# Decay sums broadcast through memory, forget columns third in the order of blocks, and first loads in one queue

## The chip, the cores and the metric

One core of a Trainium2 chip runs the whole program. The metric is the device time of one execution in microseconds (us): the median over three runs, 729.85 us for the kernel before. The profile comes from a single execution, which took 731.11 us.

## The reference, cut to what matters

Two blocks run one after the other on 256 rows of 1024 channels, all in float32: first a feed-forward layer, a chunked attention with pooling and a second feed-forward layer, then a forgetting attention ("fox") and a sparse latent attention ("dsa"). What the change touches in the arithmetic is the forgetting attention:

```python
q, k, v, f_logit, gate = _split(x @ w_in, [H * dh, H * dh, H * dh, H, D])
log_f = jax.nn.log_sigmoid((f_logit + b_f).astype(jnp.float32))
cum = jnp.cumsum(log_f, axis=1)
cum_t = jnp.transpose(cum, (0, 2, 1))
...
s = jnp.einsum('bqhd,bshd->bhqs', q_b, k).astype(jnp.float32) * scale
s = s + jnp.transpose(c_b, (0, 2, 1))[..., None] - cum_t[:, :, None, :]
s = jnp.where(kpos[None, :] <= qpos[:, None], s, -jnp.inf)
p = jax.nn.softmax(s, axis=-1).astype(v.dtype)
```

There are 8 heads of 128 channels. The score of query q and key k gets the decay sum of q, minus the decay sum of k, and a causal mask.

## The kernel before, in words

**Work and tiles.** The 256 rows are two tiles of 128 (t = 0 and 1). Every weight matrix is read once from memory, in units listed in order by `unit_list`: a unit is two blocks of 128 x 512 values (the first 8 units of all are one block each). A unit is loaded into `raw` (L209, 4 buffers) by the queue of SyncE (SP), and split by `prefetch` (L185 to L201) into a rounded part `whi` on ScalarE (ACT, L196) and the rest `wlo` on VectorE (DVE, L197), 8 buffers each. Activations are split alike (`xh`, `xl`). TensorE (PE) forms a float32 product as three fast ones: `half` (L214 to L228) issues, for each block, xl by whi, xh by wlo and xh by whi. Some small products (scores of tile 0, probabilities by values) are done in plain float32, which the profile records as two matmuls each.

**Order of the work.** `Kern` writes the instructions in one order, with side work put off: `later` and `when` push a function on a heap with a due time counted in modelled TensorE time (`now`, advanced by `mm` and `tr`), and `pump` runs what is due after each `half`. The due times stand in `DUE`. The framework's scheduler then orders the instructions of each engine by readiness in its own model; each engine runs its list strictly in that order.

**Start.** `start` (L1097) loads the channel gains by the GpSimd (POOL) queue (L1100), and by the SP queue, in turn, weights and two blocks of the transposed input `xin` (L1102 to L1104). TensorE does 40 products of zeros (L1107). `first_chunk` (L310) multiplies two blocks of `xin` by the gain into `xg` on DVE (L321), rounds it on ACT (`xh`, L324), subtracts on DVE (`xl`, L325), and issues the units. The input `x` itself, needed for the norm, is loaded after the second and fourth pair of blocks (`X_AT`, L333).

**Feed-forward.** Gate and up chunks of 512 columns alternate; the gated result is transposed through memory by POOL's queue (`regroup`, L281 to L282: `d<-hb`, then `hd<-d`), and `put_h` splits it (L238, L239) `DUE["ffn_T"]` = 6.0 after that.

**Forgetting attention** (`fox`, L687). Columns of the input projection come in the order of `FOX_CH`: two chunks of keys, two of queries, three `fox_fv` chunks of 344 (the 8 forget columns, then the values), two of gates. After the first `fox_fv` chunk `log_f` and then `cums` (L752) make the decay sums: `cq` per query row (L763), and per key in `cum`, 40 rows with the sums rounded in rows 0 to 7 and the rest in rows 32 to 39. In `scores` (L782) each head begins with a product that adds the key's decay sum to its scores in PSUM: 40 rows of a column of `E`, repeated 128 times, by `cum` (L788); then the q k products (L790, L792); then DVE adds `cq` and the mask (L793):

```python
self.mm(ps[:, i, :], E[:, h:h + 1].to_broadcast([40, P]), cum[:, 0:nk], True, False, 1)
```

There are six groups of heads (`GROUPS`): two of 4 heads for tile 0 with 128 keys, four of 2 heads for tile 1 with 256 keys. Each goes through softmax (L443, L445), a transpose (L178), the product with the values and the gate (L868), while TensorE does the gate chunks and `out_proj`.

Of the kernel before, what the change touches and what calls it, by code (L numbers as in the profile page):

```python
# [31 lines left out]
N_WARM = 40  # L32
X_AT = (1, 3)
# [12 lines left out]
def unit_list():  # L46
# [22 lines left out]
    for i, (c0, w) in enumerate(FOX_CH):  # L69
        block("fox_fv" if 4 <= i < 7 else "fox", c0, w)  # L70
# [15 lines left out]
    "ffn_T": 6.0,  # L86
# [27 lines left out]
class Kern:  # L114
# [195 lines left out]
    def first_chunk(self, u0, n, pool, gain):  # L310
# [3 lines left out]
        for t in range(2):  # L314
            self.new_xT(t)
        for kp in range(KT // 2):
            k = slice(2 * kp, 2 * kp + 2)
            xg = pool.tile([P, 2, 2, P], F32, name="xg0", bufs=2)
            for t in range(2):
                hi, lo = self.xT[t]  # L320
                nc.vector.tensor_tensor(  # L321
                    xg[:, t], self.xin[:, k, t * P:(t + 1) * P],
                    self.gain[:, gain + 2 * kp:gain + 2 * kp + 2, None].to_broadcast([P, 2, P]), op=ALU.mult)
                nc.scalar.copy(hi[:, k, :], xg[:, t])  # L324
                nc.vector.tensor_sub(lo[:, k, :], xg[:, t], hi[:, k, :].bitcast(F32))  # L325
            for i in range(2 * kp, 2 * kp + 2):
                for t in range(2):
                    self.half(accs[t], self.xT[t], u0 + i, i == 0, i == n - 1)
                self.done(u0 + i + 1)
                self.prefetch(1)  # L330
            if kp in X_AT:
                t = X_AT.index(kp)
# [38 lines left out]
    def ffn(self, u, gain, next_gain):  # L371
        nc, tc = self.nc, self.tc
        with tc.tile_pool(name="ffn", bufs=1, reuse_waits="tile") as pool:
# [10 lines left out]
            if u == 0:  # L384
                self.xin = pool.tile([P, KT, S], F32, name="xin")
                self.start()
            for j, (c0, w) in enumerate(FFN_CH):
# [3 lines left out]
                gen = self.first_chunk(u, ng, pool, gain) if u == 0 else \  # L391
# [295 lines left out]
    def fox(self, u, gain):  # L687
        self.stage = "fox"
        nc, tc, A = self.nc, self.tc, self.A
        with tc.tile_pool(name="fox", bufs=1, reuse_waits="tile") as pool:  # L690
# [6 lines left out]
            cum = pool.tile([40, S], F32R, name="cum")  # L697
            E = pool.tile([40, 8], F32R, name="E")
# [25 lines left out]
            for j in range(4):  # L724
                for t, acc in self.chunk(u, 4, gain if j == 0 else None):
                    if j == 0:
                        rs[t] = self.rstd(t)
                        hr[t], sr[t] = self.small(f"hr{t}"), self.small(f"qr{t}")
                        nc.vector.tensor_scalar(hr[t], rs[t], 0.5, None, op0=ALU.mult)
                        nc.vector.tensor_scalar(sr[t], rs[t], SC128, None, op0=ALU.mult)  # L730
                        nc.vector.scalar_tensor_tensor(self.x[t], self.x[t], rs[t], fg,
                                                       op0=ALU.mult, op1=ALU.mult)
                    if j < 2:
                        qk(acc, t, kT, [d[:, :, t * P:(t + 1) * P] for d in kTs], 4 * j, rs[t])
                    else:
                        qk(acc, t, qT, qTs if t else None, 4 * j - 8, sr[t])
                u += 4
# [14 lines left out]
            def cums():  # L752
# [17 lines left out]
            for j in range(3):  # L770
                for t, acc in self.chunk(u, 4):
                    if j == 0:
                        nc.vector.scalar_tensor_tensor(zf[:, t, :], acc[:, 0:8], rs[t], bf,
                                                       op0=ALU.mult, op1=ALU.add)
                    c0 = 8 if j == 0 else 0
                    nc.scalar.activation(v[t][:, 344 * j + c0 - 8:344 * (j + 1) - 8], acc[:, c0:344],
                                         AF.Copy, scale=rs[t])
                u += 4
                if j == 0:
                    log_f()  # L780

            def scores(t, g):  # L782
# [436 lines left out]
```

## Time and profile before

| what | value |
|---|---|
| median of 3 runs | 729.85 us (729.18 to 730.84) |
| the profiled execution's own time | 731.11 us |
| its span in the profile | 729.3 us |
| TensorE busy | 713.9 us, 98% |
| VectorE, ScalarE, GpSimd busy | 68%, 50%, 8% |
| read from and written to memory | 132.34 MB and 6.82 MB |

The span runs from the first to the last instruction of the program; the execution's own time has 1.8 us more around it. Times in the rows are in us from the start of the span, unless marked ns. PE is TensorE's matmuls, PEld its weight loads; SPq, POOLq and ACTq are the queues that issue DMAs. L12 is line 12 of the kernel; a helper's line stands for all that call it, so L163 is every matmul of `mm`.

### The profile page before, as it was taken

To read this page: it belongs to the slowest core of one execution; us is meant where nothing else is said; L and a number is where in the kernel's file an instruction comes from. 1 tells how busy PE (TensorE), PEld (TensorE's weight loads), DVE (VectorE), ACT (ScalarE), POOL (GpSimd) and SP (SyncE) were. 2 spreads that over 40 slices of the span, in tenths; PEclk is the share of its full clock that TensorE was granted. 3 is DMA by queue.
4 is the path that set the end of the run, shared out by engine and by line. 5 is a ranking of instruction groups with operands and counts; after the bars stand their busy time and mean duration, and the time that the engine had idled before them with its cause. 6 is when DMAs were issued, how large, how long until landed. Compare 5 with 4: busy or idle time off the path is not lost.

```text
span 729.3 us, 9860 instructions
## 1 busy us (share of the span) xinstructions
PE 713.9 (98%) x3608; PEld 597.6 (82%) x3608; DVE 493.7 (68%) x791; ACT 366.6 (50%) x544; POOL 58.2 (8%) x89
## 2 busy tenths in 40 slices
PE   8999999999999999999999999999999999999995
PEld 7788889888888778888889878878987889778984
DVE  6876766665647958665676556663555868998965
ACT  5654554354555736454454354554554625675820
POOL 0011110200003001101111200000000001000001
PEclk9999999999999999999999999999999999999998
DMA  7898656876735245667755767653560427533501
GB/s 261 296 320 294 228 205 217 272 266 195 264 103 204 85 149 171 209 202 252 264 200 198 275 217 229 237 158 111 193 232 29 143 66 253 208 116 116 173 1 58
DMA packets 42034, 139.80 MB, mean 192 GB/s; under 512 B 5362, under 2 KB 6530, under 8 KB 41858
## 3 DMA queue, kind: packets, MB, share of 16 engines
q1 hardware_dynamic: 37890, 127.23, 51.7%
q0 software_dynamic: 3808, 11.56, 4.6%
q8 instruction: 28, 0.46, 0.2%
q10 hardware_dynamic: 288, 0.39, 0.1%
q14 instruction: 20, 0.16, 0.1%
HBM read 132.34 MB, written 6.82 MB: 191 GB/s over the span
## 4 chain that ended last, share of the span: by engine, by line
PE 73%; DMA 11%; DVE 9%; issue 2%; ACT 2%; POOL 2%; SPq 0%; DVEq 0%; POOLq 0%; ACTq 0%
PE mm L163 63%; PE sc L163 6%; DVE wlo L197 4%; DMA raw<-in_w 3%; PE tr L178 3%; DMA hd<-d 3%; DMA d<-hb 2%; DMA rope<-in_rope 1%; POOL hrs L291 1%; ACT whi L196 1%; DMA row_final_norm<-in_final_norm 1%; PE tr L163 1%; POOL d L281 1%; DMA x<-in_x 1%; ACT s L445 0%
## 5 line engine op out<-in xcount | busy, mean ns | idle before, releaser
L197 DVE TENSOR_TENSOR wlo<-raw,whi 128x1024 fp32r<-128x1024 f32 (+3 forms) x236 | 273.9, 1175 | 86.4 <-ACT whi L196 82.8
L196 ACT CAST whi<-raw 128x1024 fp32r<-128x1024 f32 (+3 forms) x236 | 235.5, 1013 | 133.0 <-PE mm L163 82.5
L163 PE MATMUL mm<-whi,xl 128*128 128x512 f32 (+3 forms) x760 | 287.9, 380 | 1.6 <-DVE xl L325 0.8
L163 PE MATMUL mm<-wlo,xh 128*128 128x512 f32 (+3 forms) x760 | 284.1, 374 | 0.5 <-DVE wlo L197 0.2
L163 PE MATMUL mm<-whi,xh 128*128 128x512 f32 (+3 forms) x760 | 283.4, 374 | 0.0
L163 PEld LDWEIGHTS mm<-whi,xl 128*128 128x128 f32 x760 | 143.6, 189 | 25.8 <-DVE xl L325 1.0
L163 PEld LDWEIGHTS mm<-whi,xh 128*128 128x128 f32 x760 | 143.4, 189 | 24.0
L163 PEld LDWEIGHTS mm<-wlo,xh 128*128 128x128 f32 x760 | 143.7, 189 | 23.6 <-DVE wlo L197 1.8
L163 PE MATMUL mm<-whi,hl 128*128 128x512 f32 x176 | 68.7, 390 | 0.0
L163 PE MATMUL mm<-wlo,hh 128*128 128x512 f32 x176 | 68.5, 389 | 0.0
L163 PE MATMUL mm<-whi,hh 128*128 128x512 f32 x176 | 68.5, 389 | 0.0
L239 DVE TENSOR_TENSOR hl<-hd,hh 128x512 fp32r<-128x512 f32 (+1 forms) x24 | 14.5, 644 | 62.4 <-ACT hh L238 62.4
L238 ACT CAST hh<-hd 128x512 fp32r<-128x512 f32 (+1 forms) x24 | 12.8, 582 | 70.8 <-DMA hd<-d 70.8
L163 PEld LDWEIGHTS mm<-whi,hh 128*128 128x128 f32 x176 | 33.0, 188 | 6.9
L163 PEld LDWEIGHTS mm<-whi,hl 128*128 128x128 f32 x176 | 33.0, 188 | 6.8
L163 PEld LDWEIGHTS mm<-wlo,hh 128*128 128x128 f32 x176 | 33.1, 188 | 6.7
L281 POOL DMA_DIRECT2D d<-hb x48 | 26.4, 556 | 148.2 <-DVE hb L413 148.0
L400 ACT ACTIVATE th<-mm,hr 128x512 f32<-128x512 f32 (+1 forms) x24 | 15.6, 651 | 24.8 <-PE mm L163 24.8
L445 ACT ACTIVATE s<-s,nmax 128x128 f32<-128x128 f32 (+1 forms) x48 | 21.3, 446 | 12.8 <-DVE nmax L443 12.7
L291 POOL TENSOR_TENSOR rs<-ms,mhalf 128x1 f32<-128x1 f32 x10 | 6.5, 647 | 181.8 <-DVE ms L304 181.8
L402 DVE SCALAR_TENSOR_TENSOR a<-th,mm 128x512 f32<-128x512 f32 (+1 forms) x24 | 15.1, 630 | 5.2 <-ACT th L400 5.2
L411 DVE SCALAR_TENSOR_TENSOR h<-a,qr,mm 128x512 f32<-128x512 f32 (+1 forms) x24 | 16.7, 698 | 2.3 <-PE mm L163 2.3
(223 smaller groups left out, 598.6 us busy)
## 6 DMA issues: line engine op xcount, KB each, us to landing
raw<-in_w SPq DMA_DIRECT2D x208, 512.0 KB, 4.5
d<-hb POOLq DMA_DIRECT2D x40, 128.0 KB, 4.3
hd<-d POOLq DMA_DIRECT2D x10, 512.0 KB, 6.2
raw<-in_w SPq DMA_DIRECT2D x12, 344.0 KB, 3.2
raw<-in_w SPq DMA_DIRECT2D x8, 372.0 KB, 3.7
raw<-in_w SPq DMA_DIRECT2D x8, 256.0 KB, 4.6
x<-in_x SPq DMA_DIRECT2D x2, 512.0 KB, 4.6
B<-in_bias SPq DMA_DIRECT2D x1, 1024.0 KB, 5.6
```

The source lines that it names most:

```text
L163: self.nc.tensor.matmul(out, a, b, start=start, stop=stop)
L178: self.nc.tensor.transpose(out, a, self.ident[:p, :p])
L196: nc.scalar.copy(hi[:, :m], raw[:, :m])
L197: nc.vector.tensor_sub(lo[:, :m], raw[:, :m], hi[:, :m].bitcast(F32))
L238: nc.scalar.copy(hi, src)
L239: nc.vector.tensor_sub(lo, src, hi.bitcast(F32))
L281: self.nc.gpsimd.dma_start(out=d[a].rearrange("b i m -> i b m"), in_=src[32 * a:32 * a + 32])
L291: self.nc.gpsimd.tensor_tensor(out, a, self.mhalf[:, 0:1].to_broadcast(list(a.shape)), op=ALU.pow)
L400: nc.scalar.activation(th[:, :w], acc[:, :w], AF.Tanh, scale=hr[t])
L402: nc.vector.scalar_tensor_tensor(a[t][:, :w], th[:, :w], 1.0, acc[:, :w], op0=ALU.add, op1=ALU.mult)
L411: nc.vector.scalar_tensor_tensor(h[:, :w], a[t][:, :w], qr[t], acc[:, :w], op0=ALU.mult, op1=ALU.mult)
L445: nc.scalar.activation(s[:, h, :], s[:, h, :], AF.Exp, bias=m[:, h:h + 1], accum_out=l[:, col + h:col + h + 1])
```

## The change

Decay sums: the `E` by `cum` product goes, with the tiles `E`, `Ef`, `cum` and the load of `Ef`. `cums` writes the negated key sums to memory and reads them back repeated over 128 rows into `ck` (8 heads by 256 keys), all by POOL's queue; POOL adds the mask into `ck0` (tile 0) and into the second half of `ck`. The score's addition on DVE reads `ck` in place of the mask. Order: the first `fox_fv` chunk moves from fifth to third place, ahead of the query chunks. Start: the gains are loaded by ACT's queue; SP's queue alternates single blocks of `xin` with weights; the input split is one ACT and one DVE instruction per block (`first_x`); 28 products of zeros in place of 40. Products: `half` issues xh by whi first. `put_h` is due at 9.5 in place of 6.0.

```diff
-N_WARM = 40
-X_AT = (1, 3)
+N_WARM = 28
+X_AT = (3, 5)
...
-FOX_CH = [(1024, 512), (1536, 512), (0, 512), (512, 512),
-          (0, 344), (344, 344), (688, 344),
-          (3080, 512), (3592, 512)]
+FOX_CH = [("fox", 1024, 512), ("fox", 1536, 512), ("fox_fv", 0, 344),
+          ("fox", 0, 512), ("fox", 512, 512),
+          ("fox_fv", 344, 344), ("fox_fv", 688, 344),
+          ("fox", 3080, 512), ("fox", 3592, 512)]
...
-    "ffn_T": 6.0,
+    "ffn_T": 9.5,
...
-            self.mm(o, xl[:, kk, :], hi[:, k, c], first and k == 0, False, 1)
-            self.mm(o, xh[:, kk, :], lo[:, k, c], False, False, 1)
-            self.mm(o, xh[:, kk, :], hi[:, k, c], False, last and k == nk - 1, 1)
+            self.mm(o, xh[:, kk, :], hi[:, k, c], first and k == 0, False, 1)
+            self.mm(o, xl[:, kk, :], hi[:, k, c], False, False, 1)
+            self.mm(o, xh[:, kk, :], lo[:, k, c], False, last and k == nk - 1, 1)
...
-    def first_chunk(self, u0, n, pool, gain):
+    def first_x(self, k, t, gain):
+
+        hi, lo = self.xT[t]
+        g = self.gain[:, gain + k:gain + k + 1]
+        src = self.xin[:, k, t * P:(t + 1) * P]
+        self.nc.scalar.activation(hi[:, k, :], src, AF.Copy, scale=g)
+        self.nc.vector.scalar_tensor_tensor(lo[:, k, :], src, g, hi[:, k, :].bitcast(F32), op0=ALU.mult, op1=ALU.subtract)
+
+    def first_chunk(self, u0, n, gain):
...
+        for i in range(KT):
             for t in range(2):
...
+                self.half(accs[t], self.xT[t], u0 + i, i == 0, i == n - 1)
+            self.done(u0 + i + 1)
+            if i + 2 < KT:
                 for t in range(2):
...
+                    self.first_x(i + 2, t, gain)
+            self.prefetch(1)
+            if i in X_AT:
+                t = X_AT.index(i)
                 nc.sync.dma_start(out=self.x[t], in_=self.A["x"][t * P:(t + 1) * P, :])
...
-            cum = pool.tile([40, S], F32R, name="cum")
-            E = pool.tile([40, 8], F32R, name="E")
+
+            ck = pool.tile([P, 8, S], F32, name="ck")
+            ck0 = pool.tile([P, 8, P], F32, name="ck0")
...
-            Ef = pool.tile([40, 8], F32, name="Ef")
-            nc.sync.dma_start(out=Ef, in_=A["E"])
-            nc.gpsimd.tensor_copy(E, Ef)
-            nc.gpsimd.memset(cum.bitcast(F32), 0.0)
...
-                nc.scalar.copy(cum[0:8, :], ps[0:8, 0:S])
-                nc.vector.tensor_sub(cs, ps[0:8, 0:S], cum[0:8, :].bitcast(F32))
-                nc.gpsimd.tensor_copy(cum[32:40, :], cs)
+                nc.scalar.activation(cs, ps[0:8, 0:S], AF.Copy, scale=-1.0)
+                d = self.dp.tile([8, S], F32, name="ck")
+                nc.gpsimd.dma_start(out=d, in_=cs)
+                diag = self.cmask[:, None, P:S].to_broadcast([P, 8, P])
+                for k in range(2):
+                    c = slice(k * P, (k + 1) * P)
+                    nc.gpsimd.dma_start(out=ck[:, :, c], in_=d[None, :, c].to_broadcast([P, 8, P]))
+                nc.gpsimd.tensor_tensor(ck0, ck[:, :, 0:P], diag, op=ALU.add)
+                nc.gpsimd.tensor_tensor(ck[:, :, P:S], ck[:, :, P:S], diag, op=ALU.add)
                 self.fire(("fox", "cum"))
...
+            qk_chunks((0, 1))
+            fv_chunks((0,))
+            log_f()
+            qk_chunks((2, 3))
+            fv_chunks((1, 2))
...
-                    self.mm(ps[:, i, :], E[:, h:h + 1].to_broadcast([40, P]), cum[:, 0:nk], True, False, 1)
                     if t == 0:
-                        self.mm(ps[:, i, :], qT[:, h, :], kT[:, h, :], False, True)
+                        self.mm(ps[:, i, :], qT[:, h, :], kT[:, h, :], True, True)
                     else:
-                        self.mm3(ps[:, i, :], qTs, kTs, False, True, (slice(None), h), (slice(None), h))
+                        self.mm3(ps[:, i, :], qTs, kTs, True, True, (slice(None), h), (slice(None), h))
                     nc.vector.scalar_tensor_tensor(s[:, i, :], ps[:, i, :], cq[t][:, h:h + 1],
-                                                   self.cmask[:, S - nk:S], op0=ALU.add, op1=ALU.add)
+                                                   (ck if t else ck0)[:, h, :], op0=ALU.add, op1=ALU.add)
...
-        nc.gpsimd.dma_start(out=self.gain, in_=A["gain"])
-        for kp in range(KT // 2):
-            self.load(kp)
-            for c in ((slice(0, P), slice(P, S)) if kp == 0 else (slice(0, S),)):
-                nc.sync.dma_start(out=self.xin[:, 2 * kp:2 * kp + 2, c], in_=A["xT"][:, 2 * kp:2 * kp + 2, c])
+        nc.scalar.dma_start(out=self.gain, in_=A["gain"])
+        for k in range(4):
+            nc.sync.dma_start(out=self.xin[:, k, :], in_=A["xT"][:, k, :])
+            self.load(k)
+        for k in (4, 6):
+            nc.sync.dma_start(out=self.xin[:, k:k + 2, :], in_=A["xT"][:, k:k + 2, :])
+        warm = self.small("warm")
+        nc.scalar.activation(warm, self.mhalf, AF.Tanh)
...
-        self.prefetch(2)
+        for t in range(2):
+            self.new_xT(t)
+        self.first_x(0, 0, gain)
+        self.prefetch(1)
+        self.first_x(0, 1, gain)
+        self.first_x(1, 0, gain)
+        self.prefetch(1)
+        self.first_x(1, 1, gain)
```

## Rows read from the trace of the kernel before

**Rows 1.** The page: busy time of TensorE, share of the span, instructions.
```profile
PE 713.9 (98%) x3608; PEld 597.6 (82%) x3608; DVE 493.7 (68%) x791; ACT 366.6 (50%) x544; POOL 58.2 (8%) x89
```

**Rows 2.** Stretches: length, busy PE PEld DVE ACT POOL, then PEclk, DMA share, GB/s.
```profile
10.00:20.00 10.00, 10.00 (x41) 8.04 (x40) 7.41 (x19) 6.96 (x14) 0.56 (x1) 0.91 0.87 309
...
0.00:26.20 26.20, 23.54 (x113) 18.52 (x113) 16.41 (x34) 15.77 (x26) 1.47 (x6) 0.93 0.80 266
```

**Rows 3.** Timeline of the start: start, duration, instruction, [idle before it, releaser].
```profile
1.01 4.32 PE L1107 MATMUL tr<-zero 128*128 128x128 bf16 x40 [1.01 <-DVE zero L1119]
...
3.40 0.62 ACT L196 CAST whi<-raw 128x512 fp32r<-128x512 f32 x1 [1.17 <-DMA raw<-in_w]
...
4.73 0.43 DVE L321 TENSOR_TENSOR xg<-xin,gain 128x256 f32<-128x256 f32 x1 [3.77 <-DMA gain<-in_gain]
...
6.14 0.50 PE L163 MATMUL mm<-whi,xl 128*128 128x512 f32 x1 [0.81 <-DVE xl L325]
...
9.46 0.63 PE L163 MATMUL mm<-wlo,xh 128*128 128x512 f32 x1
```

**Rows 4.** The chain that ended last, in order of time: start, length, what.
```profile
26.18 138.32 PE mm L163 x654
...
492.62 5.50 PE mm L163 x24
...
586.10 13.65 PE mm L163 x60
```

**Rows 5.** PE timeline, scores of tile 0.
```profile
541.89 0.32 PE L163 MATMUL sc<-cum,E 40*128 40x128 f32 x1
...
543.06 0.48 PE L163 MATMUL mm<-whi,xl 128*128 128x512 f32 x1
543.47 0.32 PE L163 MATMUL sc<-cum,E 40*128 40x128 f32 x1
```

**Rows 6.** PE timeline, one head of tile 1.
```profile
557.33 0.38 PE L163 MATMUL sc<-cum,E 40*128 40x256 f32 x1
...
558.10 0.39 PE L163 MATMUL mm<-whi,xl 128*128 128x512 f32 x1
```

**Rows 7.** PE timeline, probabilities by values.
```profile
560.12 1.05 PE L163 MATMUL sc<-v,pT 128*128 128x128 f32 x8
560.93 0.48 PE L163 MATMUL mm<-whi,xh 128*128 128x512 f32 x1
```

**Rows 8.** Busy time by engine from the first score to the last transpose of tile 1.
```profile
541.80:585.40 43.60, 43.60 (x237) 35.01 (x237) 31.17 (x64) 20.95 (x50) 0.00 (x0) 1.00 0.32 109
```

**Rows 9.** Group of DVE instructions, 541 to 570 us: busy us, mean ns, idle before.
```profile
L793 DVE SCALAR_TENSOR_TENSOR s<-sc,cq,cst 128x128 f32<-128x128 f32 x8 | 2.8, 350 | 4.5 <-PE sc L163 4.5
```

**Rows 10.** Groups of POOL instructions over the whole span.
```profile
L291 POOL TENSOR_TENSOR hrs<-hms,mhalf 128x8 f32<-128x8 f32 x4 | 7.5, 1876 | 32.2 <-DVE hms L499 32.2
L291 POOL TENSOR_TENSOR rs<-ms,mhalf 128x1 f32<-128x1 f32 x10 | 6.5, 647 | 181.8 <-DVE ms L304 181.8
...
L923 POOL COPY kid<-y 128x128 f32<-128x128 f32 x2 | 0.7, 354 | 17.2 <-DVE y L915 13.9 <-DVE y L914 3.3
```

**Rows 11.** DMA issues: queue, count, KB each, median us from issue to landing.
```profile
xin<-in_xT SPq DMA_DIRECT2D x2, 128.0 KB, 3.5
...
rope<-in_rope SPq DMA_DIRECT2D x1, 96.0 KB, 8.8
```

**Rows 12.** DVE timeline: the last copy of the decay sums, and the first score.
```profile
528.21 0.16 DVE L763 COPY cq<-tr 128x8 f32<-128x8 f32 x1
...
542.67 0.35 DVE L793 SCALAR_TENSOR_TENSOR s<-sc,cq,cst 128x128 f32<-128x128 f32 x1 [1.90 <-PE sc L163]
```

**Rows 13.** Timelines of PE and ACT: waits near layer borders and for `hd`.
```profile
283.84 0.50 PE L163 MATMUL mm<-whi,xl 128*128 128x512 f32 x1 [0.29 <-DVE xl L245]
...
423.10 0.71 ACT L238 CAST hh<-hd 128x256 fp32r<-128x256 f32 x2 [6.68 <-DMA hd<-d]
...
436.70 1.25 PE L178 MATMUL tr<-cst,x 128*128 128x128 f32 x8 [0.93 <-DVE x L433]
```

More of the change, by code (lines that the diff above doesn't have):

```diff
@@ L68, in unit_list @@
     ffn(2)
-    for i, (c0, w) in enumerate(FOX_CH):
-        block("fox_fv" if 4 <= i < 7 else "fox", c0, w)
+    for m, c0, w in FOX_CH:
+        block(m, c0, w)
     for n in range(2):
@@ L385, in ffn @@
                 self.xin = pool.tile([P, KT, S], F32, name="xin")
-                self.start()
+                self.start(gain)
             for j, (c0, w) in enumerate(FFN_CH):
@@ L390, in ffn @@
                 a = [None, None]
-                gen = self.first_chunk(u, ng, pool, gain) if u == 0 else \
+                gen = self.first_chunk(u, ng, gain) if u == 0 else \
                     self.chunk(u, ng, gain if j == 0 else None)
@@ L722, in qk, with qk_chunks @@
                 self.later(DUE["fox_T"], go)
[L724 to L737, printed above, removed]
+            def qk_chunks(js):
+                nonlocal u
+                for j in js:
+                    for t, acc in self.chunk(u, 4, gain if j == 0 else None):
+                        if j == 0:
+                            rs[t] = self.rstd(t)
+                            hr[t], sr[t] = self.small(f"hr{t}"), self.small(f"qr{t}")
+                            nc.vector.tensor_scalar(hr[t], rs[t], 0.5, None, op0=ALU.mult)
+                            nc.vector.tensor_scalar(sr[t], rs[t], SC128, None, op0=ALU.mult)
+                            nc.vector.scalar_tensor_tensor(self.x[t], self.x[t], rs[t], fg,
+                                                           op0=ALU.mult, op1=ALU.mult)
+                        if j < 2:
+                            qk(acc, t, kT, [d[:, :, t * P:(t + 1) * P] for d in kTs], 4 * j, rs[t])
+                        else:
+                            qk(acc, t, qT, qTs if t else None, 4 * j - 8, sr[t])
+                    u += 4
             zf = pool.tile([P, 2, 8], F32, name="zf")
@@ L764, in cums, with fv_chunks @@
                 cs = pool.tile([8, S], F32, name="cs")
-                nc.scalar.copy(cum[0:8, :], ps[0:8, 0:S])
-                nc.vector.tensor_sub(cs, ps[0:8, 0:S], cum[0:8, :].bitcast(F32))
-                nc.gpsimd.tensor_copy(cum[32:40, :], cs)
-                self.fire(("fox", "cum"))
[L770 to L780, printed above, removed]
+                nc.scalar.activation(cs, ps[0:8, 0:S], AF.Copy, scale=-1.0)
[7 more added lines that the diff above has]
+                nc.gpsimd.tensor_tensor(ck[:, :, P:S], ck[:, :, P:S], diag, op=ALU.add)
+                self.fire(("fox", "cum"))
+            def fv_chunks(js):
+                nonlocal u
+                for j in js:
+                    for t, acc in self.chunk(u, 4):
+                        if j == 0:
+                            nc.vector.scalar_tensor_tensor(zf[:, t, :], acc[:, 0:8], rs[t], bf,
+                                                           op0=ALU.mult, op1=ALU.add)
+                        c0 = 8 if j == 0 else 0
+                        nc.scalar.activation(v[t][:, 344 * j + c0 - 8:344 * (j + 1) - 8], acc[:, c0:344],
+                                             AF.Copy, scale=rs[t])
+                    u += 4
+            qk_chunks((0, 1))
[3 more added lines that the diff above has]
+            fv_chunks((1, 2))
             def scores(t, g):
@@ L1095, in dsa, with start @@
         return u
-    def start(self):
+    def start(self, gain):
         nc, A = self.nc, self.A
-        nc.gpsimd.dma_start(out=self.gain, in_=A["gain"])
-        for kp in range(KT // 2):
-            self.load(kp)
-            for c in ((slice(0, P), slice(P, S)) if kp == 0 else (slice(0, S),)):
-                nc.sync.dma_start(out=self.xin[:, 2 * kp:2 * kp + 2, c], in_=A["xT"][:, 2 * kp:2 * kp + 2, c])
+        nc.scalar.dma_start(out=self.gain, in_=A["gain"])
[6 more added lines that the diff above has]
+        nc.scalar.activation(warm, self.mhalf, AF.Tanh)
         ps = self.bank("tr")
@@ L1119, in run @@
         nc.vector.memset(self.zero, 0.0)
-        warm = self.small("warm")
-        nc.scalar.activation(warm, self.mhalf, AF.Tanh)
         self.ident, self.tri, self.ones = (cst[:, i * P:(i + 1) * P] for i in range(3))
```

20 lines of the change are left out of this document (1 added, 19 removed).

## The prediction

> **What bounds the kernel now.** The page comes first: TensorE is busy for 98% of the span, the next engine, DVE, for 68% [rows 1]. So a change pays only where it takes work off TensorE or closes one of its few waits. The windows and the timeline of the start show where it is not yet fed: in the first 26.2 us the DMA engines are busy for a share of 0.80 [rows 2], and the first real product starts at 6.14 us, behind an input split that began at 4.73 us, when the gains had landed; the first weights were being rounded at 3.40 us already [rows 3]. Soon after, a 512-column matmul takes 0.63 us [rows 3] where the same takes 0.39 us later [rows 6]: the lower of the clock's two levels, and a mean granted clock of 0.93 over the 26.2 us [rows 2]. At full clock 24 of them take 5.50 us, a spacing of 0.229 us [rows 4]. The chain of waits shows TensorE alone from 26.18 us on for 138 us [rows 4]. The third place is the score stage of the forgetting attention, where the view to read is the distance between starts, for busy time hides it: pipelined matmuls overlap, and TensorE looks busy throughout.
>
> **Score stage: the E products.** 16 of them go, 8 of 128 keys and 8 of 256. For tile 0 the pattern from one E to the second next is two heads and one 512-column product: 543.47 - 541.89 = 1.58 us [rows 5]. Without E it holds that product, 0.229 us, and four records of q k at the price of an undisturbed 128-column product; eight of these take 560.93 - 560.12 = 0.81 us, 0.10 each [rows 7]. 0.23 + 0.40 = 0.63, so 0.95 per pattern, four patterns: 3.8 us. For tile 1 one head takes 558.10 - 557.33 = 0.77 us [rows 6]; its three products of 256 columns at half the 512 spacing are 0.34, so E costs 0.43, eight heads: 3.4 us. Sum 7.2 us, all on TensorE. Where a 40-row E follows a 128-row product it also starts late, which may give another 0.7 us (16 x 0.04); upper end 7.9.
>
> What is late next there: every head's scores go to DVE (0.350 us for 128 keys [rows 9], the new one with a tensor of the same size for the mask, so the same), and heads of one group share a PSUM bank, so the next head's products wait for DVE. The stretch up to the last transpose is 43.6 us with DVE busy 31.2 and ACT 21.0 [rows 8]; without E it would be 36.4, DVE at 86%. The out projection then has 60 products left, 48 of them tile 1's own [rows 4], so 12 x 0.229 = 2.7 us could be pulled forward as cover. If the chain through softmax did not shorten at all, 43.6 - 36.4 - 2.7 = 4.5 us would be a stall: lower end 2.7 us gained. Since DVE still has spare time and weight splits run 8 units ahead, I take 6.2.
>
> **The key sums through memory.** The new chain is: ACT negates (nearest row 0.6 us at 128 x 512 [rows 3], here 8 x 256), POOL writes 8 KB to memory, reads it back twice as 512 KB in 512-byte pieces, and adds the mask twice over 1024 columns. No row shows these. Landing: between 3.5 us (a load of 512-byte pieces) and 8.8 us (the slowest) [rows 11]; three in sequence 10.5 to 26.4. The adds: a copy of 128 columns takes 354 ns, so 8 times that, 2.8 us each, is the near price; the far one is the power function, (1876 - 647) / 7 = 176 ns a column [rows 10]. I take the copy, an add being one pass as well: 0.6 + 18 + 5.6 = 24 us. Cover: from the last decay sum to the first score 542.67 - 528.21 = 14.5 us [rows 12], plus the two query chunks that now follow, 96 products x 0.229 = 22 us: 36.5. The forget chunk itself is only moved, at the same 48 products. So nothing waits, with 12 us to spare; below zero is excluded, as no work ended on the old chain. POOL loses two casts and a fill, gains three issues and two adds; until the layer norm nothing else stands in its queue. DVE loses one subtraction, SP the load of `Ef`. The broadcast puts 1 MB into the load stream: at most eight 128 KB loads of such pieces, 8 x 3.5 = 28 us of landing [rows 11], while 8 split units ahead last about 8 x 2.7 = 22 us and the weights still get a share; I price it at nothing. The new tiles push the row loads to later addresses, last used for the gated results, which were split by 423.8 us, before the layer's border at 436.7 us [rows 13].
>
> **Start.** The gains leave POOL's queue for ACT's, which issues them before its table load; SP sends one input block, then one weight block. Next late is the first weights' rounding: 3.40 + 0.62 = 4.0 us [rows 3], a little later as 128 KB of input now stand ahead, so first products at about 4.6: 1.5 us earlier. The 28 zero products end near 1.01 + 28 x 0.108 = 4.0 (4.32 us for 40 [rows 3]), so the pause ahead of real work shrinks from 0.81 to about 0.6. The low clock cost 0.07 x 26.2 = 1.8 us of full speed [rows 2]; with xh by whi first, each unit needs `wlo` only two products (0.46 us) later, so pauses shorten and I count half of it or a little more back. DVE drops eight multiplications of `xg` (0.43 us in the row [rows 3]). The limit is the DMA: 20% of 26.2 us is 5.2 us idle [rows 2], about 2 of it before anything can land, so 3.2 us at most. I take 2.5, range 0 to 3.2.
>
> **Feed-forward and borders.** With `put_h` later, ACT blocks less on `hd` (6.68 us in one place); that block delayed weights up to the wait of 0.93 us at 436.7, which I expect to go [rows 13]. The new order of products hides a late `xl` by one product: 0.23 of the 0.29 us at 283.84 [rows 13]. Together 1.1, range 0 to 2. If the later split were late instead, the down projection's last units would wait, but those stand at the end of its first chunk.
>
> **Sum.** 6.2 + 2.5 + 1.1 = 9.8 us. The profiled execution took 731.11 us, 1.26 above the median of 729.85: 721.3 for such an execution, 720.0 for the median.
>
> **A rule against this.** The next sentences the rest can do without. The Trainium skill, page "TensorE: Matmul & The Clock Gate", section "Wait — 56ns, not 53.3ns?", has a warm matmul's start-to-start as its columns over 2.4 GHz plus about 2.5 ns; by it the E products cost an estimated 1.3 us, and the sum would be 4.9 and the median 725.0. The trace disagrees: two E products of 128 keys cost 0.95 us [rows 5, 7], not 0.11.
>
> **Rivals.**
> 1. *The softmax chain holds the score stage.* DVE at 86% [rows 8] speaks for it, its idle time before the scores (4.5 us, waiting for TensorE [rows 9]) against. 2.7 + 2.5 + 1.1 = 6.3: 723.5 us.
> 2. *The start gains nothing*, since bytes set it or the clock falls again. For: DMA share 0.87 from 10 to 20 us [rows 2]. Against: 5.2 us idle. 6.2 + 1.1 = 7.3: 722.5 us.
> 3. *E's time is not E's*: what stands behind it is a change of bank or a DVE release that the q k product inherits. Then E is worth 8 x 0.10 + 8 x 0.12 = 1.8 us, in all 5.4: 724.5 us. Against: the 0.81 us block begins in a PSUM bank without such a delay [rows 7]. By the rule above it would come out close to this.
> 4. *Slower: the scores wait for `ck`.* Place: DVE's first score; its queue then holds weight splits. Price: the two adds on POOL. It decides once an add exceeds about 9 us, since 36.5 - 18.6 leaves 18 for both; it costs more than the 9.8 gained at 20 ns a column, between copy and power function [rows 10]: ready at 18.6 + 40 = 58.6 us, tile 1's scores are due 15 us after tile 0's, at 51.5, and tile 0's wait for the first add is 18.6 + 20 - 36.5 = 2, so about 7 us; at 30 ns 18.6 + 61 - 51.5 = 28 us: 748 us.
> 5. *It does not do what it says*: the scheduler's new order loses about what it gains, 729.5 us.
>
> **Numbers.** Chances: forecast 0.62, rival 1 0.15, rival 2 0.10, rival 3 0.06, rival 5 0.04, rival 4 0.03. Range: upward to rival 3, 725.0; downward the upper ends, 7.9 + 3.2 + 2.0 = 13.1 give 716.7, so 716.0. A measurement here tells 0.2%, 1.5 us, from no change. Faster by more: the forecast and rivals 1 to 3, 0.93; same, rival 5, 0.04; slower, rival 4, 0.03.
>
> **What would show it.** Right: in the score stage heads follow each other at 0.2 us of products with no gap; busy PE time falls by about 7 us; first product near 4.6 us and full clock by 9; `ck` written some 10 us before the first score; no wait at the second layer's border. Wrong: DVE's scores waiting for POOL or a DMA, TensorE waiting for transposes of the last groups, the lower clock past 12 us, or a spacing of 0.25 us ahead of the q k products as before.

## The result, and the profile after

The changed kernel takes **723.47 us** (median of 4 runs, 722.39 to 726.33) where the kernel before, run beside it, took 730.35 us (729.18 to 730.86): ratio **0.9917**, 95% interval 0.9900 to 0.9935. It is faster, by just under one per cent; the time lies inside the predicted range, 3.5 us above the predicted 720.0. The profiled execution took 723.93 us (span 722.1). Line numbers shift, by different amounts: `mm` is L164, the rounding of weights L197 and L198, the transposes L179, the scores L803.

The page's first part: TensorE is 7.4 us less busy [rows 1], POOL 4.1 us more.

```profile
PE 706.5 (98%) x3580; PEld 593.9 (82%) x3580; DVE 492.1 (68%) x790; ACT 369.4 (51%) x552; POOL 62.3 (9%) x90
```

The timeline of the **start** [rows 3]. The gains land 0.71 us earlier (4.02 for 4.73), but the first weights are rounded 1.22 us later (4.62 for 3.40), and the first product starts 0.87 us earlier (5.27 for 6.14). A 512-column product takes 0.63 us, the lower of the clock's two levels, from there to 9.3 us; then, at 19.01 us, TensorE waits 0.52 us for weights.

```profile
4.02 0.69 ACT L316 ACTIVATE xh<-xin,gain 128x128 fp32r<-128x128 f32 x2 [1.35 <-DMA gain<-in_gain]
...
5.27 0.79 PE L164 MATMUL mm<-whi,xh 128*128 128x512 f32 x1 [1.09 <-ACT whi L197]
...
8.85 0.63 PE L164 MATMUL mm<-whi,xh 128*128 128x512 f32 x1
...
9.62 0.39 PE L164 MATMUL mm<-whi,xl 128*128 128x512 f32 x1
...
19.01 0.50 PE L164 MATMUL mm<-whi,xh 128*128 128x512 f32 x1 [0.52 <-ACT whi L197]
```

Before, the first products were at the upper level [rows 3]; the lower one came at 8.2 us and lasted to 11.9:

```profile
8.61 0.63 PE L163 MATMUL mm<-whi,xh 128*128 128x512 f32 x1
...
11.97 0.39 PE L163 MATMUL mm<-wlo,xh 128*128 128x512 f32 x1
```

The windows of the changed kernel [rows 2]: the DMA engines are busier (0.87 for 0.80), from 10 us on the clock is at its upper level throughout, and yet TensorE is busy for 9.48 us between 10 and 20 us, where it was busy for all 10. The clock of 1.00 in the first of the two rows misses the stretch up to 9.3 us, in which the products took 0.63 us.

```profile
0.00:26.20 26.20, 23.32 (x103) 18.10 (x104) 15.27 (x37) 17.77 (x36) 1.31 (x6) 1.00 0.87 284
10.00:20.00 10.00, 9.48 (x42) 7.29 (x40) 7.23 (x19) 7.64 (x17) 0.56 (x1) 1.00 0.90 280
```

The timeline of the **scores** [rows 5, 6]: four q k records (two heads), two 512-column products, and again; for tile 1 one head between 558.68 and 559.03. From pair to pair it is 0.91, 1.04 and 0.93 us; less two products, 0.46, that is 0.45, 0.58 and 0.47 for two heads, 0.50 in the mean; before it was 1.58 - 0.23 = 1.35. In the longest of the three the weight load of the pair waits 0.26 us for DVE (`s`) and starts with its product.

```profile
542.22 0.60 PE L164 MATMUL sc<-kT,qT 128*128 128x128 f32 x4
...
543.12 0.56 PEld L164 LDWEIGHTS sc<-kT,qT 128*128 128x128 f32 x4 [0.26 <-DVE s L803]
543.13 0.73 PE L164 MATMUL sc<-kT,qT 128*128 128x128 f32 x4
...
544.17 0.63 PE L164 MATMUL sc<-kT,qT 128*128 128x128 f32 x4
...
545.10 0.64 PE L164 MATMUL sc<-kT,qT 128*128 128x128 f32 x4
...
558.68 0.28 PE L164 MATMUL sc<-kTsh,qTsl 128*128 128x256 f32 x1
...
559.03 0.40 PE L164 MATMUL mm<-wlo,xh 128*128 128x512 f32 x1
```

**What is new stands at the second layer's border.** First the same place before, from DVE's timeline: xl of the first tile (468.62), behind it the multiplication of x by final_norm's row, which waits for that row.

```profile
468.62 0.68 DVE L245 TENSOR_TENSOR xl<-xg,xh 128x512 fp32r<-128x512 f32 x1
470.37 1.28 DVE L731 SCALAR_TENSOR_TENSOR x<-x,rs,row_final_norm 128x1024 f32<-128x1024 f32 x1 [1.07 <-DMA row_final_norm<-in_final_norm]
```

After, in the timelines of DVE and TensorE: the row is issued at 462.10, 2.3 us earlier than before (464.37), but on DVE the multiplication now stands ahead of xl. It waits for the row, xl waits behind it, and TensorE waits 2.23 us for xl. Then six matmuls at 0.63 us pass before the upper clock is back; the window of that stretch, the last row, has a granted clock of 0.50.

```profile
468.54 1.28 DVE L730 SCALAR_TENSOR_TENSOR x<-x,rs,row_final_norm 128x1024 f32<-128x1024 f32 x1 [2.74 <-DMA row_final_norm<-in_final_norm]
469.75 0.69 DVE L246 TENSOR_TENSOR xl<-xg,xh 128x512 fp32r<-128x512 f32 x1
...
467.78 0.48 PE L164 MATMUL mm<-whi,xh 128*128 128x512 f32 x1
470.49 0.80 PE L164 MATMUL mm<-whi,xl 128*128 128x512 f32 x1 [2.23 <-DVE xl L246]
...
473.64 0.44 PE L164 MATMUL mm<-wlo,xh 128*128 128x512 f32 x1
...
470.40:473.60 3.20, 3.12 (x7) 2.49 (x8) 3.20 (x6) 0.62 (x1) 0.00 (x0) 0.50 0.49 157
```

The chain that ended last names the row too, from its issue to its landing:

```profile
462.10 6.36 DMA row_final_norm<-in_final_norm
```

The **way of the key sums** on POOL and the first score on DVE: the two adds take 2.39 and 2.40 us and are done at 519.85, 22.9 us before the first score.

```profile
506.21 0.57 POOL L766 DMA_DIRECT2D ck<-cs  x1 [40.65 <-ACT cs L764]
508.40 1.82 POOL L770 DMA_DIRECT2D ck<-ck  x2 [1.62 <-PE tr L179]
515.02 2.39 POOL L771 TENSOR_TENSOR ck<-ck,cst 128x1024 f32<-128x1024 f32 x1 [4.80 <-DMA ck<-ck]
517.45 2.40 POOL L772 TENSOR_TENSOR ck<-ck,cst 128x1024 f32<-128x1024 f32 x1
...
542.71 0.61 DVE L803 SCALAR_TENSOR_TENSOR s<-sc,cq,ck 128x128 f32<-128x128 f32 x2 [1.66 <-PE sc L164]
```

Taken together by the shift of the same instruction between the two traces: the first gate activation stands at 18.86 instead of 19.30 us (0.44 earlier); at 374 us the lead is 0.86, at 463 us 2.4. Behind the border it is gone (between 0.4 ahead and 1.1 behind at 490 us, 0.43 behind at 534), and behind the score stage it is a lead of 6.5, 7.2 at the end.

### The profile page after: what moved, and what is told of

Same layout as the page of the kernel before. It is cut to its first block, busy times and chain, and to the rows that moved or that the text cites. A ratio compares the mean times of both kernels' runs of the same rounds, so it can differ in the third digit from the quotient of the medians.

```text
span 722.1 us, 9816 instructions
## 1 busy us (share of the span) xinstructions
PE 706.5 (98%) x3580; PEld 593.9 (82%) x3580; DVE 492.1 (68%) x790; ACT 369.4 (51%) x552; POOL 62.3 (9%) x90
## 4 chain that ended last, share of the span: by engine, by line
PE 88%; DVE 5%; DMA 3%; ACT 2%; issue 1%; SPq 0%; POOL 0%; DVEq 0%; POOLq 0%; ACTq 0%
PE mm L164 79%; PE sc L164 5%; PE tr L179 3%; DVE wlo L198 2%; DMA raw<-in_w 1%; DMA row_final_norm<-in_final_norm 1%; PE tr L164 1%; ACT whi L197 1%; DMA xin<-in_xT 1%; ACT s L445 0%; DVE sel L983 0%; DVE xl L317 0%; DVE sel L992 0%; DVE s L534 0%; POOL hrs L292 0%
## 5 line engine op out<-in xcount | busy, mean ns | idle before, releaser
L198 DVE TENSOR_TENSOR wlo<-raw,whi 128x1024 fp32r<-128x1024 f32 (+3 forms) x236 | 274.6, 1178 | 84.8 <-ACT whi L197 74.9
L197 ACT CAST whi<-raw 128x1024 fp32r<-128x1024 f32 (+3 forms) x236 | 235.7, 1014 | 126.0 <-PE mm L164 76.4
L164 PE MATMUL mm<-whi,xh 128*128 128x512 f32 (+3 forms) x760 | 289.3, 381 | 1.7 <-ACT whi L197 1.6
L164 PE MATMUL mm<-whi,xl 128*128 128x512 f32 (+3 forms) x760 | 284.9, 375 | 2.2 <-DVE xl L246 2.2
L164 PE MATMUL mm<-wlo,xh 128*128 128x512 f32 (+3 forms) x760 | 284.0, 375 | 0.1
L164 PEld LDWEIGHTS mm<-whi,xh 128*128 128x128 f32 x760 | 144.0, 189 | 25.7 <-ACT whi L197 3.0
L164 PEld LDWEIGHTS mm<-whi,xl 128*128 128x128 f32 x760 | 144.2, 190 | 25.0 <-DVE xl L246 2.7
L164 PEld LDWEIGHTS mm<-wlo,xh 128*128 128x128 f32 x760 | 143.9, 189 | 25.3 <-DVE wlo L198 1.3
L164 PE MATMUL mm<-whi,hh 128*128 128x512 f32 x176 | 68.7, 390 | 0.0
L164 PE MATMUL mm<-whi,hl 128*128 128x512 f32 x176 | 68.5, 389 | 0.0
L164 PE MATMUL mm<-wlo,hh 128*128 128x512 f32 x176 | 68.5, 389 | 0.0
L240 DVE TENSOR_TENSOR hl<-hd,hh 128x512 fp32r<-128x512 f32 (+1 forms) x24 | 14.5, 644 | 53.3 <-ACT hh L239 53.3
L164 PEld LDWEIGHTS mm<-wlo,hh 128*128 128x128 f32 x176 | 33.0, 188 | 6.9
L164 PEld LDWEIGHTS mm<-whi,hh 128*128 128x128 f32 x176 | 33.1, 188 | 6.7
L164 PEld LDWEIGHTS mm<-whi,hl 128*128 128x128 f32 x176 | 33.1, 188 | 6.7
L292 POOL TENSOR_TENSOR lr<-ve,mhalf 128x1 f32<-128x1 f32 x4 | 4.0, 992 | 167.8 <-DVE ve L640 167.8
```

The source lines that it names most:

```text
L164: self.nc.tensor.matmul(out, a, b, start=start, stop=stop)
L197: nc.scalar.copy(hi[:, :m], raw[:, :m])
L198: nc.vector.tensor_sub(lo[:, :m], raw[:, :m], hi[:, :m].bitcast(F32))
L240: nc.vector.tensor_sub(lo, src, hi.bitcast(F32))
L292: self.nc.gpsimd.tensor_tensor(out, a, self.mhalf[:, 0:1].to_broadcast(list(a.shape)), op=ALU.pow)
```

## The experiments

Twelve kernels ran. Ratios are to the kernel before in the same series (729.6 to 729.8 us); one hundredth is 7.3 us. By the intervals given, a difference between two of these ratios is known to some 2 us.

**1. E back (e1).** The changed kernel with the 16 products of `cum` and `E` back, and no `ck`.

```diff
+self.mm(ps[:, i, :], E[:, h:h + 1].to_broadcast([40, P]), cum[:, 0:nk], True, False, 1)
-                   (ck if t else ck0)[:, h, :], op0=ALU.add, op1=ALU.add)
+                   self.cmask[:, S - nk:S], op0=ALU.add, op1=ALU.add)
```

> The changed kernel (723.5 us) with the E products put back and the sums through memory left out; all else as changed. Theory A (an E product costs what its neighbours' spacings showed, 7 to 8 us in all): 730.5 to 731.5 us, about the time of the kernel before. Rival, E worth its columns alone (1.3 to 1.8 us): 725 us. Rival, the softmax chain holds the stage (2.7 us gained by taking E away): 726 us.

Measured: 729.85 us (727.43 to 732.49), ratio 1.0005 (0.9989 to 1.0021). That is just under the range of theory A and about 4 us above the nearer rival. Against 0.9917 the E products are worth 0.0088, 6.4 us, known to some 2 us. The border stall was there as well, but smaller: 1.64 us of TensorE, and no lower clock behind it.

The traces give a sharper price, since one stretch can be taken alone: from the last but one of the activations that write the values (`v`, on ACT), ahead of the scores, to the first product of the layer norm behind them (on DVE). In e1 it lasts 592.15 - 531.46 = 60.69 us and in the kernel before 594.76 - 534.12 = 60.64; in the changed kernel it lasts 53.69 and in e2 (below) 53.73. By that the 16 products cost 7.0 us. The two ends in e1, then in the changed kernel:

```profile
531.46 0.55 ACT L781 ACTIVATE v<-mm,rs 128x344 f32<-128x344 f32 x1 [2.40 <-PE mm L164]
592.15 1.41 DVE L644 SCALAR_TENSOR_TENSOR x<-x,mv,row_ln_g 128x512 f32<-128x512 f32 x2
...
534.55 0.55 ACT L783 ACTIVATE v<-mm,rs 128x344 f32<-128x344 f32 x1 [2.40 <-PE mm L164]
588.24 1.41 DVE L644 SCALAR_TENSOR_TENSOR x<-x,mv,row_ln_g 128x512 f32<-128x512 f32 x2
```

**2. E with 128 rows (e5).** The same, with `E` and `cum` of 128 rows, the added ones zero.

```diff
-cum = pool.tile([40, S], F32R, name="cum")
+cum = pool.tile([128, S], F32R, name="cum")
```

> As the run with the E products put back, but E and the sums have 128 rows, zeros below row 40: same columns, same products, only the number of rows differs. Theory A (the cost is the change between a 40-row and a 128-row tile, which keeps the weight load from running ahead): about 0.11 us an E product, so 6 us less than with 40 rows, 724.5 to 725.5 us. Rival (the cost is the repeated column of E as weights, or the bank): no less than with 40 rows, about 731 us.

Measured: 725.0 us (724.36 to 726.59), ratio 0.9939 (0.9915 to 0.9963). That lies in the range of theory A. The same products with over three times the rows cost 0.0022, 1.6 us, in place of 6.4; 1.6 alone cannot be told from nothing, but the stretch of the score stage lasts 55.45 us here, 1.8 us more than without E and 5.2 less than with 40 rows. The view that shows what differs is TensorE's weight loads, beside its products. With 40 rows, in e1 (loads, then products): no load runs for 0.24 us ahead of that of E though no releaser is named, the load of the q k product starts 0.26 us behind that of E, and the loads begin with their products (543.04 and 543.05, 543.30 and 543.30), not ahead of them.

```profile
542.37 0.18 PEld L164 LDWEIGHTS sc<-cum,E 40*128 40x128 f32 x1 [0.24 <-issue]
...
543.04 0.18 PEld L164 LDWEIGHTS sc<-cum,E 40*128 40x128 f32 x1
543.30 0.30 PEld L164 LDWEIGHTS sc<-kT,qT 128*128 128x128 f32 x2
...
543.05 0.32 PE L164 MATMUL sc<-cum,E 40*128 40x128 f32 x1
543.30 0.49 PE L164 MATMUL sc<-kT,qT 128*128 128x128 f32 x2
```

With 128 rows, in e5, the first load of E starts at 541.11, 0.23 us before its product. Later ones wait for DVE (`s`) and start with theirs, as at 542.27; but the next load follows 0.11 us behind, and the next product 0.06 to 0.17 us behind that of E:

```profile
541.11 0.19 PEld L164 LDWEIGHTS sc<-cum,E 128*128 128x128 f32 x1
...
542.27 0.18 PEld L164 LDWEIGHTS sc<-cum,E 128*128 128x128 f32 x1 [0.19 <-DVE s L802]
542.38 0.30 PEld L164 LDWEIGHTS sc<-kT,qT 128*128 128x128 f32 x2
...
541.34 0.22 PE L164 MATMUL sc<-cum,E 128*128 128x128 f32 x1
541.40 0.44 PE L164 MATMUL sc<-kT,qT 128*128 128x128 f32 x2
...
542.27 0.33 PE L164 MATMUL sc<-cum,E 128*128 128x128 f32 x1
542.44 0.44 PE L164 MATMUL sc<-kT,qT 128*128 128x128 f32 x2
```

So in these rows no weight load is started ahead into or out of the 40-row tile. The row count is worth three quarters of what E cost (5.2 of 7.0 us by the stretch); the rest, 1.8 us, is what the products cost with full rows.

**3. The row by POOL's queue (e2).** POOL issues final_norm's row at 410.88 us, long before the border; everything else as in the changed kernel.

```diff
-fg = self.row(pool, "final_norm")
+fg = self.row(pool, "final_norm", q=nc.gpsimd)
```

> The changed kernel with the final norm row loaded by POOL's queue in place of SP's, so that it need not stand behind weight loads. Theory A (TensorE's pause of 2.2 us at 468 us and the low clock after it come from DVE waiting for that row): the pause goes, 3 to 4 us less, 719.5 to 720.5 us. Rival (the pause only moves to the next late thing, the weights or the split): 722.5 to 723.5 us.

Measured: **721.0 us** (720.13 to 721.39), ratio **0.9875** (0.9853 to 0.9898): 3.1 us better, half a us above the range of theory A and below that of the rival; it is the base of the runs below. The two traces run side by side up to the border (460.97 and 460.91 us for the same addition on DVE) and stand 4.06 us apart behind it (484.05 and 479.99 for the same activation on ACT). DVE's timeline shows the same order with no wait:

```profile
465.40 1.28 DVE L730 SCALAR_TENSOR_TENSOR x<-x,rs,row_final_norm 128x1024 f32<-128x1024 f32 x1
466.59 0.68 DVE L246 TENSOR_TENSOR xl<-xg,xh 128x512 fp32r<-128x512 f32 x1
```

In the window from 460 to 480 us TensorE is busy for all 20 us at the upper clock; the changed kernel has 17.77 us and a mean clock of 0.91 there.

**4. The multiplication put off (e2_defer).** The row stays in SP's queue.

```diff
-nc.vector.scalar_tensor_tensor(self.x[t], self.x[t], rs[t], fg,
-                               op0=ALU.mult, op1=ALU.mult)
+self.later(8.0, lambda t=t: nc.vector.scalar_tensor_tensor(
+    self.x[t], self.x[t], rs[t], fg, op0=ALU.mult, op1=ALU.mult))
```

> Base is the changed kernel itself (723.5 us): final_norm's row stays in SP's queue. Here only the multiplication of x by it (DVE) is emitted 8 units of the planner's time later, so that it no longer stands ahead of xl on DVE. Theory: the stall at the border (2.23 us of TensorE and the fall of the clock behind it) comes from DVE's queue order alone: 720.5 to 721.5, no wait between 465 and 475 us. Rival: the late row, or the multiplication's 1.28 us in another place, costs the same elsewhere: 723.0 to 724.0.

Measured: 724.09 us (722.86 to 726.52), ratio 0.9926 (0.9909 to 0.9943): no gain. The expectation missed, because the edit did not do what it was for. The scheduler put tile 0's multiplication ahead of xl again; only tile 1's, which had nothing to wait for, went behind (474.39).

```profile
469.82 1.28 DVE L730 SCALAR_TENSOR_TENSOR x<-x,rs,row_final_norm 128x1024 f32<-128x1024 f32 x1 [2.46 <-DMA row_final_norm<-in_final_norm]
471.02 0.68 DVE L246 TENSOR_TENSOR xl<-xg,xh 128x512 fp32r<-128x512 f32 x1
```

It shows that the stall stays as long as that one instruction stands there and its row is late; with the row early (e2) it stands there and costs nothing. Which part of the change moved it ahead is open: E back (e1) leaves it ahead.

**5. No key sums (e12).** The scores get the mask alone; nothing goes through memory.

```diff
-nc.gpsimd.dma_start(out=d, in_=cs)
-    nc.gpsimd.dma_start(out=ck[:, :, c], in_=d[None, :, c].to_broadcast([P, 8, P]))
-nc.gpsimd.tensor_tensor(ck0, ck[:, :, 0:P], diag, op=ALU.add)
...
```

> Base is the changed kernel with final_norm's row in POOL's queue (721.0 us, 0.9875 of before). Here the keys' decay sums are left out of the scores: nothing is written to memory and read back, POOL adds no mask, and DVE's operation on the scores adds the mask alone. It prices the way through memory, which the prediction set at nothing. Theory: it lies beside other work, 721.0, within 0.7 us. Rival: the 1 MB that is read back pushes weights back, or the stores and adds cost something in place: 719.0 to 720.2.

Measured: 720.75 us (719.76 to 721.64), ratio 0.9873 (0.9858 to 0.9887), as the theory had it: the way through memory costs nothing that can be told.

**6. The forget columns in fifth place (e6).**

```diff
-qk_chunks((0, 1))
-fv_chunks((0,))
-log_f()
-qk_chunks((2, 3))
+qk_chunks((0, 1, 2, 3))
+fv_chunks((0,))
+log_f()
```

> Same base (721.0 us). Here the forget columns go back to fifth place among the blocks; the way through memory stays. From the last decay sum to the first score there are then 14.5 us. Theory (measured chain of the changed kernel, 506.2 to 519.9 us, about 14 us): just in time, 721.0 to 722.0, at most 1 us of waiting ahead of the first scores. Rival (the estimate of the prediction, 24 us): the scores wait some 9.5 us, of which 2.7 us can be covered by products pulled forward: 727 to 728, ratio 0.996, with a wait of DVE's first score for POOL.

Measured: 724.81 us (722.38 to 726.46), ratio 0.9926 (0.9907 to 0.9945), 3.7 us more than the base: between the two expectations. The timeline of all engines shows the scores too early for `ck`: the first add ends at 541.14, DVE's first scores start at 542.14, behind a weight split, and TensorE, whose next scores wait for DVE to read the last, stands for 1.51 us. The last 1.0 of it is the split's, not that of `ck`.

```profile
538.75 2.39 POOL L771 TENSOR_TENSOR ck<-ck,cst 128x1024 f32<-128x1024 f32 x1 [6.51 <-DMA ck<-ck]
...
540.58 1.64 DVE L198 TENSOR_TENSOR wlo<-raw,whi 128x1024 fp32r<-128x1024 f32 x1 [2.93 <-PE sc L164]
...
541.11 3.35 POOL L772 TENSOR_TENSOR ck<-ck,cst 128x1024 f32<-128x1024 f32 x1
542.14 0.60 DVE L802 SCALAR_TENSOR_TENSOR s<-sc,cq,ck 128x128 f32<-128x128 f32 x2
542.54 0.75 PE L164 MATMUL sc<-kT,qT 128*128 128x128 f32 x4 [1.51 <-DVE s L802]
```

The wait explains 1.5 us of the 3.7; the profiled execution also lost some 2 us in its start, whose code is that of the base, and how much of the rest is the place was not settled.

**7. The start: 40 zero products (e3), x later (e10), all of it as before (e14).** e3 stands on the changed kernel, the two others on e2.

```diff
 e3:  -N_WARM = 28
      +N_WARM = 40
 e10: -X_AT = (3, 5)
      +X_AT = (5, 7)
 e14: start, first_chunk, N_WARM, X_AT and the place of the table load as before
```

> The changed kernel with 40 zero products in place of 28. Theory A (28 end 1.1 us before the first product, and the clock is low until 9.5 us; with 40 it is granted as the first product starts): 1.0 to 1.9 us less, 721.6 to 722.5 us. Rival (bytes set the start): the clock is high but the time the same, 723.5 us, with pauses for weights in place of the slow products.

> Same base (721.0 us). Here the two loads of x (512 KB each) are issued behind units 5 and 7 instead of 3 and 5. Theory (the first 26 us are set by bytes): the pauses for whi between 18 and 26 us, 0.5 to 0.6 us each, come later or shrink, since up to 1 MB less (3.5 us at 300 GB/s) stands ahead of the weights: 719.5 to 720.5, and the instruction that stood at 26 us comes 0.5 to 1.5 us earlier. Rival: the pauses only move, since the same bytes have to come before the queue is 8 units ahead: 721.0.

> Same base (721.0 us). Here the whole start goes back to that of before: gains by POOL's queue, input blocks by pairs, the split by way of xg, 40 zero products, x behind units 1 and 3, the table load first; the order of products stays. Theory (traces of before and after: the same instruction at 19 us stands 0.44 us earlier, 0.15 to 0.4 later on): 721.2 to 721.6. Rival 1 (the prediction's 2.5 us): 723.5. Rival 2: what came on top between 280 and 463 us (0.4 and 1.5 us) hangs on the start's order too: 722.5 to 723.2, with the wait at 435 us back.

Measured: e3 724.58 us (722.44 to 728.94), ratio 0.9930 (0.9908 to 0.9953), not better than 0.9917; e10 722.14 us (720.1 to 723.34), 0.9892 (0.9875 to 0.9909), not better than 0.9875; e14 **720.97 us** (720.32 to 721.28), 0.9879 (0.9866 to 0.9892), the same as the base. The theories of e3 and e10 are refuted; e14 came out just under its theory's range, and both its rivals fall. In e3 the products are at the upper clock from 6.8 us rather than 9.6, and the time that they saved went into waits for the next weights (TensorE's timeline):

```profile
6.79 0.39 PE L164 MATMUL mm<-whi,xh 128*128 128x512 f32 x1
...
18.83 0.50 PE L164 MATMUL mm<-whi,xh 128*128 128x512 f32 x1 [0.60 <-ACT whi L197]
```

In all twelve traces with the new start TensorE waits for weights between 18.7 and 20.4 us, by 0.5 to 1.7 us; in the two with the old start (before and e14) it does not wait there. What the loads brought in the first 26.2 us, from the DMA view; before:

```profile
DMA packets 3294, 6.97 MB, mean 266 GB/s; under 512 B 345, under 2 KB 972, under 8 KB 3293
```

The changed kernel:

```profile
DMA packets 3450, 7.45 MB, mean 284 GB/s; under 512 B 508, under 2 KB 1143, under 8 KB 3449
```

By 20 us the new order has moved no more bytes (5.17 MB for 5.33), and more of its packets are small; by 26.2 us it has moved 0.48 MB more. But the second load of x, 512 KB that the first products do not need, is issued at 15.46 us instead of 21.06, so that about as much of the gain is not weights. The first gate activation starts between 18.6 and 20.2 us in all fourteen traces, whatever the clock did: at 19.30 and 19.45 with the old start, at 19.47 in the median with the new one.

**8. Order of products (e7), due time (e4), both (e13)**, each on e2.

```diff
 e7:  -self.mm(o, xh[:, kk, :], hi[:, k, c], first and k == 0, False, 1)
      +self.mm(o, xl[:, kk, :], hi[:, k, c], first and k == 0, False, 1)
      ...
 e4:  -    "ffn_T": 9.5,
      +    "ffn_T": 6.0,
 e13: both
```

> Same base (721.0 us). Here the three products of a unit go back to the old order, xl by whi first. Theory (prediction): a border loses 0.23 us where xl is the last to come (three layer borders), and at the start the first product waits for xl instead of whi, 0.3 to 0.5 us: 721.8 to 722.2. Rival 1: nothing, since the start is set by bytes and the borders wait for something else: 721.0. Rival 2: the old order is better, since wlo is rounded behind whi and may be used one product later now: 720.5.

> Base is the changed kernel with final_norm's row in POOL's queue (721.0 us, 0.9875 of before). Here ffn_T, the due time of the feed-forward's transposes, goes back from 9.5 to 6.0; all else stays. Theory (my step on the feed-forward): the wait of 0.93 us at 436.7 us of before comes back, with the stretch around it 1.3 us as in before: 722.3 to 722.6, ratio near 0.9895, and ACT's idle time for hd goes back from 61 towards 71 us. Rival: that wait went because the weights now come in another order, and the due time is worth nothing: 721.0, no wait of TensorE between 430 and 440 us.

> Same base (721.0 us). Here both go back, the order of a unit's products (xl first) and ffn_T (6.0); each alone changed nothing (721.1 and 720.7). Theory: together they change nothing either, 721.0, and TensorE has no wait of 0.9 us before the border at 435 us, so the wait in before came from the timing of the weights there. Rival: either of the two alone covers that wait, and with both undone it comes back: 722.3 to 722.8.

Measured: e7 721.14 us (720.93 to 722.03), ratio 0.9882 (0.9867 to 0.9897); e4 720.69 us (719.35 to 721.7), 0.9872 (0.9855 to 0.9889); e13 722.8 us (721.85 to 724.63), 0.9905 (0.9891 to 0.9920). Each alone is worth nothing that can be told, against the theories of e7 and e4. In e7 the wait for xl at the first border is back (0.28 us), as [rows 13] had it. In no trace is TensorE's wait of 0.93 us near 436 us back. Both together cost 2.2 us by the medians, with intervals that overlap: the time of e13's rival, without the wait that was to make it. The profiled execution of e13 had a stretch of low clock between 20 and 30 us (mean 0.83). That sum stays inconclusive.

## Why the prediction was right, and where a step failed

**The E products: right, with the price read and its cause not seen.** 6.2 us were taken; the medians give 6.4 (e1), known to some 2 us, the stretch of the score stage 7.0. So the 7.2 of the working nearly held, and the 1.0 that was taken off for the chain through softmax was not lost. Inside, tile 0 gave 1.35 - 0.50 = 0.85 us per pair and not 0.95, since four q k records cost 0.50 rather than 0.40; tile 1's head now takes 0.35 us of 0.77 before, 0.42 for E as worked out. 4 x 0.85 + 8 x 0.42 = 6.8. Rival 1 (the softmax chain holds the stage) would have kept E at 2.7, and rival 3 (E's time is not E's) at 1.8: both fall with e1, though a wait of the q k load for DVE, as rival 3 had it, is there (0.26 us at 543.12). The lateness of a 40-row product was given 0.7 us at most; by e5 the row count is three quarters of the price. That 723.47 is just the time that rival 1 gave, 723.5, is chance.

**The rule that was weighed.** By the stretch, 40-row E costs 7.0 us and 128-row E 1.8 us (e1, e5). The start-to-start rule of the Trainium skill, page "TensorE: Matmul & The Clock Gate", section "Wait — 56ns, not 53.3ns?", from which the prediction had an estimated 1.3 us, comes near the 128-row run and not the 40-row ones. The same page says in "Step-by-step: what each phase is for" that the row count does not matter for the weight load; its duration is indeed 0.18 to 0.19 us in either case here, but when it starts is not the same.

**The key sums: right at nothing** (e12). The chain took 14 us where 24 were estimated (adds 2.4 for 2.8; the landings some 9 for 18, for the two reads went out together), and the spare was 22.9 us, not 12. Rival 4 needed an add of 9 us; its own working makes it 7 us at 20 ns a column, less than the 9.8 that it says is exceeded there. In the fifth place, with 14.5 us of cover [rows 12], the run is 3.7 us slower and TensorE waits 1.5 us, a third of it for `ck` (e6): the third place is worth having, for how much is open.

**The start: wrong, rival 2 right.** The failed step is "The limit is the DMA: 20% of 26.2 us is 5.2 us idle", and from it 2.5 us. Undoing the whole start changes 0.0004, 0.3 us (e14), known to some 2 us. Idle share of the DMA engines was read as bytes that could come earlier and save time. The engines did become busier (0.87 for 0.80), but no more had come by 20 us, and what more had come by 26.2 us is about the size of one load of x. The first product came 0.87 us earlier, where 1.5 were counted, and that was handed back as waits for weights (0.52 us at 19.01). The half of the clock's 1.8 us that was counted back did not come either: some 4 us of lower clock, 5.3 to 9.3 us, stand in place of 3.7, 8.2 to 11.9. Both terms were priced as if nothing stood behind them. That it is the bytes that set the start fits e3, whose faster products saved nothing, but it is argued: no run took bytes away, and e10, with x later, gained nothing.

**The border: the step that cost most.** The prediction had the row loads "last used for the gated results, which were split by 423.8 us, before the layer's border", and expected no wait at the second layer's border: a term put at nothing. It asked when the row could be issued (right: even earlier), not what stands behind its reader in DVE's list. The row is late in both kernels (it lands at 470.4 us before, at 468.5 after); before, only the multiplication waited for it, and now xl and TensorE do. The price is 0.0042, 3.1 us, by the medians of e2, and 4.0 us by the two traces. It is the mechanism of rival 5, a new order of the scheduler that loses, at a third of its size. In the trace of before the sign was there: the multiplication waited 1.07 us for that DMA, one place behind xl.

**Feed-forward and borders: direction right, cause open.** 1.1 us were taken. The waits of before that are gone (0.93 us near 436, 0.77 and 0.12 behind 474, 0.29 at 283.84 us) make 2.1 us. With the border mended (e2) the gain is 0.0125, 9.1 us, as much as E's 7.0 and these 2.1 together. But the old start, the old order and the old due time take back only 0.3, 0.5 and -0.2 us one at a time; that a later `put_h` removes the first of the waits, as the prediction argued, e4 does not bear out. The combination was tried once (e13), without a clear answer.

**The sum**, from the shift of the same instructions between the traces of before and after: 2.4 us up to the border (start, feed-forward and waits, where 3.6 were forecast), -2.9 at the border (0 forecast), 7.0 in the score stage (6.2), 0.7 behind it (0): 7.2, the difference of the two profiled executions (731.11 and 723.93); the medians differ by 0.0083, 6.1 us. The forecast of 9.8 would have been about right for e2 (9.1), but by luck: a start that was too dear against E and other waits too cheap.

## What to carry to other kernels

Before a late load is called harmless, look at what stands behind its first reader on that engine: an instruction with no hurry of its own can hold one that TensorE waits for, and a new schedule can swap the two without a word in the diff. Before an earlier first product or a higher clock at the start is counted as a gain, ask whether the weights behind it come earlier too; here they did not, and the time went into waits for them. Price a product of few rows amid full-height ones by the distance between starts, and try padding it to 128 rows first: here that gives three quarters of what removing it does.

## What the hardware showed that was not expected

A 40-row product between 128-row ones costs 0.3 us more than its 128-row twin (7.0 - 1.8 = 5.2 us over 16); in the rows of e1 neither its weight load nor the next one starts ahead. A pause of TensorE of 2.23 us was followed by a stretch at the lower clock (granted 0.50): from 470.49 to 473.64 us seven products started, in 3.15 us instead of 7 x 0.23 = 1.6. That is another 1.5 us, so the wait cost two thirds as much again as it lasted. Pauses of 1.64 us (e1) and 1.74 us (e5) at the same place were not followed by it. Where POOL's add and a weight split of DVE overlapped (e6), the add took 3.35 us instead of 2.39 and the split 1.64 instead of 1.23.
